# Where z's factors are loaded from, and in what steps z is squared and split, in an FP32 encoder block

## The chip, the core and the metric

The kernel runs on one core of a Trainium2 chip. The metric is the device time of one execution in microseconds. The kernel before took 1945.86 us, the median of three runs (1943.88 to 1946.81).

## The reference, cut to what matters

One layer of an encoder block on 512 positions of width 2048, all in float32. The change lies in its last part, the MLP with a squared ReLU:

```python
m = rms_norm(h, mlp_pre_gain[l])
z = jnp.square(jax.nn.relu(jnp.einsum("bsd,df->bsf", m, w_up[l])))
z = jnp.einsum("bsf,fd->bsd", z, w_down[l])
h = h + rms_norm(z, mlp_post_gain[l])
```

w_up is 2048 x 8192 and w_down 8192 x 2048. Ahead of it stand a projection w_in, two causal convolutions with gates, a LayerNorm, and a projection w_out with a norm.

## The kernel before

**Float32 by parts.** Each operand is split into a high part (a copy rounded to fp32r, made by ACT, L235 for weights) and a low part (the value less the high part, made by DVE, L239), and a block's product is three matmuls: high by low, low by high, high by high.

**Seven products for eight.** Most of w_out, w_up and w_down is multiplied by a scheme of the Strassen-Winograd kind: for two tiles of a weight and two halves of the positions, seven products of sums take the place of eight ("a seven"). The weight sums are DVE's (L163 for w_up, L195 for w_down). For w_up a product is 24 matmuls 128x256 (L292), and `by_seven` runs them in the order r11, t2, t1, r21, t3, r22, t4. p1 (the product r11) is copied out of its bank by ACT (L341, `tmp<-bank`); DVE forms u = p1 + t2 and v = u + t1 (L333, `tmp<-tmp,bank`); the sum into the upper half of c2 (L333, `slot<-tmp,bank`) reads the bank of t3, the "seventh", onto which t4 is then accumulated, so that t4 cannot begin before that sum is done. w_up's first eight tiles are done plainly ("plain pairs", two tiles each, evacuated by `plain_z`), the other 56 as 28 sevens. For w_down, `wide_seven` runs chunks 1 to 7 with two sevens each, a product of 24 matmuls 128x512 (L928), and chunk 0 plainly at the end.

**Order of the work.** The order is the program's. `product` first takes its weights: `take` prepares those of the next products ahead (weight sums, L235, L239). Then `run_pending` issues what has been put in the list `pending`: evacuations of the product before and steps of z. Then come the matmuls. Each engine works through its own instructions in that order.

**z.** The output of a pair of tiles (`zt`, 128x1024) goes to `keep_z`, which puts steps into the list `z_jobs`: Relu, Square and the high part in one step on ACT (L783, L784, L789), then the store of the high part (a DMA on ACT's queue, L804) with the low part (DVE, L333 `slot<-slot,slot`), then the store of the low part with z's own sums (three DVE instructions, not for the first chunk), and the same split and stores for those sums. `up_product` takes one step a product, two when more than six wait. In the first seven of w_up each product also takes two of the eight "late sums": splits by ACT and DVE of 128x256 (L94, L95) which t4's right side needs.

**Factors.** A chunk of z (4 pairs of tiles) is read back from DRAM as factors, t1, t2, r11, t3, r22, t4, r21 in the order of use, each in a high and a low tile of 512 KB (`load_factor`, L893: 14 loads for each of chunks 1 to 7 and 8 for chunk 0). They are issued by SP, on whose queue stand also all loads of raw weights (L122) and of w_down's last blocks of a seven (L207). A tile's place comes from a pool of 43 slots that weights, factors and z share; a load waits for its place. The first chunk's factors are issued at two points of the last `by_seven` and after it; each later chunk's in the second seven of the chunk before, `after` a product.

The profile's names are those of the pools: `raw` a raw weight, `slot` a 4 KB place, `tmp` a scratch tile, `bank` a PSUM bank.

Of the kernel before, what the change touches and what calls it, by code (L numbers as in the profile page):

```python
# [10 lines left out]
AF = mybir.ActivationFunctionType  # L11
# [16 lines left out]
N_UP = FF // P  # L28
# [30 lines left out]
def encoder_block(  # L59
    ctx: ExitStack, tc: tile.TileContext, x, par, gain, w_in, w_out, w_up, w_down, out  # L60
):
    nc = tc.nc
# [239 lines left out]
    def full_tile(parts, moving):  # L302
        ps = bank()
        products(ps, [(block(parts[k // HALF], k % HALF), both(moving[k])) for k in range(KT)])
        return ps
# [30 lines left out]
    def run_pending():  # L336
        while pending:
            pending.popleft()()

    def evacuate(f, *args):  # L340
        pending.append(lambda: f(*args))  # L341
# [11 lines left out]
    def product(right, blocks, onto=None):  # L353
        (part,) = W.take(1, 3)
        run_pending()
        ps = bank(TOK) if onto is None else onto
        products(ps, [(block(part, i), right(i)) for i in range(blocks)], onto=onto is not None)
        return ps

    def by_seven(product, c1, c2, done1, done2, step=lambda n: None):  # L360


        p1, u, v = scratch(TOK), scratch(TOK), scratch(TOK)
        first = product("r11")
        evacuate(nc.scalar.activation, p1, first, AF.Copy)
        evacuate(add, u, p1, product("t2"))
        evacuate(add, v, u, product("t1"))
        product("r21", first)
        evacuate(nc.scalar.activation, c1[:, lower], first, AF.Copy)
        seventh = product("t3")  # L370
        evacuate(add, c2[:, upper], v, seventh)
        evacuate(step, 1)
        evacuate(add, c1[:, upper], v, product("r22"))
        evacuate(done1, c1)
        evacuate(step, 3)
        product("t4", seventh)
        evacuate(add, c2[:, lower], u, seventh)
        evacuate(done2, c2)
# [22 lines left out]
    class Sum:  # L401
# [3 lines left out]
        def add(self, t):  # L405
            if self.total is None:
                self.total = new(stats, [P, self.cols], F32, "sum")
                nc.gpsimd.tensor_copy(self.total, t)
            else:
                nc.gpsimd.tensor_tensor(self.total, self.total, t, op=ALU.add)  # L410
# [182 lines left out]
    for kind, j, m in in_plan[START:]:  # L593
# [3 lines left out]
        ps = full_tile(parts, u)  # L597
# [48 lines left out]
    for m in range(START, OUT_SEVEN[0]):  # L646
        parts = W.take(2, 2)
        run_pending()
        ps = full_tile(parts, mixed)
        evacuate(keep_output, m, ps, scratch())  # L650
    for m in OUT_SEVEN:
        by_seven(
            lambda name, onto=None: product(mixed_factor[name], HALF, onto),
            *(scratch() for _ in range(2)),
            *((lambda c, m=n: keep_output(m, c, c)) for n in (m, m + 1)),
        )
# [111 lines left out]
    WIDE_ORDER = ("t1", "t2", "r11", "t3", "r22", "t4", "r21")  # L768
# [4 lines left out]
    )  # L773
    z_jobs = deque()

    def keep_z(n, zt):


        c, i = divmod(n, PAIRS)
        made = {}  # L780

        def squared():
            nc.scalar.activation(zt, zt, AF.Relu)  # L783
            nc.scalar.activation(zt, zt, AF.Square)  # L784
            high(zt, 0)

        def high(value, g):
            made["hi", g] = slot([P, 4, TOK], F32R)
            nc.scalar.activation(  # L789
                made["hi", g].rearrange("p f w -> p (f w)"),  # L790
                value.rearrange("p a b -> p (a b)"), AF.Copy,
            )

        def rest(value, g):
            made["lo", g] = slot([P, 4, TOK], F32R)
            add(
                made["lo", g].rearrange("p f w -> p (f w)"),
                value.rearrange("p a b -> p (a b)"),
                made["hi", g].rearrange("p f w -> p (f w)").bitcast(F32), ALU.subtract,
            )  # L800

        def store(g, h):
            part = made["lo" if h else "hi", g]
            nc.scalar.dma_start(z_parts[c, g, h, i], part.bitcast(F32))  # L804

        def sums():
            t = made["t"] = slot([P, 4, TOK])
            q = zt.rearrange("p a (b w) -> p (a b) w", b=2)
            add(t[:, :2, :], q[:, 1::2, :], q[:, :2, :], ALU.subtract)
            add(t[:, 2, :], q[:, 3, :], t[:, 0, :], ALU.subtract)  # L810
            add(t[:, 3, :], q[:, 2, :], t[:, 2, :], ALU.subtract)

        z_jobs.append([squared])
        z_jobs.append([lambda: store(0, 0), lambda: rest(zt, 0)])
        if c == 0:
            z_jobs.append([lambda: store(0, 1)])
            return
        z_jobs.append([lambda: store(0, 1), sums])
        z_jobs.append([lambda: high(made["t"], 1)])
        z_jobs.append([lambda: store(1, 0), lambda: rest(made["t"], 1)])  # L820
        z_jobs.append([lambda: store(1, 1)])

    def z_job(n):
        for _ in range(min(n, len(z_jobs))):
            pending.extend(z_jobs.popleft())

    t12, t3, t4 = [], [], []
# [17 lines left out]
    def last_right_sum(i):  # L845
        split(t4[i // 4][:, i % 4, :], *both(mlp_in[2 * i], upper))
# [11 lines left out]
    def plain_z(n, pss, zt):  # L858

        for i, ps in enumerate(pss):  # L860
            nc.scalar.activation(zt[:, i, :], ps, AF.Copy)
        keep_z(n, zt)

    for n in range(START // 2):
        evacuate(lambda n=n: plain_z(n, pss[2 * n : 2 * n + 2], slot([P, 2, S])))
    n = HALF // (UP_PLAIN - START)
    for m in range(START, UP_PLAIN):
        parts = W.take(2, 2)
        run_pending()
        ps = full_tile(parts, mlp_in)  # L870
# [7 lines left out]
    late_sums = deque(range(HALF))  # L878

    def up_product(name, onto=None):  # L880
        for _ in range(2):
            if late_sums:
                pending.append(lambda i=late_sums.popleft(): last_right_sum(i))
        z_job(2 if len(z_jobs) > 6 else 1)
        return product(right_factor[name], HALF, onto)

    factors = {}
# [1 line left out]
    def load_factor(c, name):  # L889
        f = FACTORS.index(name)  # L890
        for h in range(2):
            t = factors[c, name, h] = slot([P, PAIRS, TOK], F32R)
            nc.sync.dma_start(  # L893
                t.rearrange("p i w -> p (i w)").bitcast(F32),
                z_dram.rearrange("p (n w) -> n p w", w=PAIRS * TOK)[((c * 2 + f // 4) * 4 + f % 4) * 2 + h],
            )

    def load_first(n):
        for name in WIDE_ORDER[3 * (n == 3) : 3 + (n == 3)]:
            load_factor(1, name)  # L900

    for m in range(UP_PLAIN, N_UP, 2):
        zt = slot([P, 2, S])
        by_seven(
            up_product,
            zt[:, 0, :],
            zt[:, 1, :],
            lambda c: None,
            lambda c, m=m, zt=zt: keep_z(m // 2, zt),
            load_first if m == N_UP - 2 else lambda n: None,  # L910
        )


# [21 lines left out]
    def right_blocks(c, name, i):  # L935
        return [factors[c, name, h][:, i, :] for h in range(2)]

    def wide_seven(c, t, after):


# [16 lines left out]
        for q, (name, group, to, first) in enumerate((  # L957
            ("t1", "p5", "c2 upper", True),
            ("t2", "p6", "c1 upper", True),
            ("r11", "p1", "all but c1 lower", True),  # L960
            ("t3", "p6", "c2 upper", False),
            ("r22", "p5", "c1 upper", False),
            ("t4", "p6", "c2 lower", True),
            ("r21", "p1", "c1 lower", True),
        )):
            z_job(1)
            parts = W.take(2, 4)
            run_pending()
            if group not in banks:
                banks[group], onto = [bank() for _ in range(2)], False  # L970
            else:
                onto = True
            for j, ps in enumerate(banks[group]):
                for i in range(PAIRS):
                    wide(
                        ps, right_blocks(c, name, i), j, parts[i // 2], i % 2,
                        i == 0 and not onto, i == PAIRS - 1, True,
                    )
                evacuate(accumulate, c == 1 and first, sums[to][j], ps)
            after(q)  # L980

    run_pending()
    for name in WIDE_ORDER[4:]:
        load_factor(1, name)
    for c in range(1, N_CHUNK):
        following = WIDE_ORDER if c + 1 < N_CHUNK else FACTORS[:4]
        c_next = (c + 1) % N_CHUNK

        def after(q):
            if q > 0 and q - 1 < len(following):  # L990
                load_factor(c_next, following[q - 1])

        for t in range(0, N_WIDE, 2):
            wide_seven(c, t, after if t == 2 else lambda q: None)
        if c_next:
            load_factor(c_next, following[-1])

    def wide_tile(t, c, blocks, step):

# [140 lines left out]
    for b in range(TB):  # L1140
        gained = {}
        for t in range(N_WIDE):
            run_pending()
            ps = bank()
# [90 lines left out]
```

## Time and profile before

| | us |
|---|---|
| median of three runs | 1945.86 |
| the profiled execution | 1949.1 |
| its span in the trace | 1947.4 |
| mean granted clock of TensorE in it | 0.993 |

In the trace the stage of w_up's sevens lies from 715.8 us to 1295.1 us, and w_down's from 1294.9 us on. A row of a timeline gives the start from the span's start, the duration, the engine, the line, what is written and read, and in brackets the idle time ahead of it and what ended it. SPq and ACTq are the engines' DMA issues.

### The profile page before, as it was taken

The numbers are of one execution on the slowest core, as the hardware profiler recorded it, in microseconds if no ns is written. First come the engines' busy times: TensorE is split into PE (matmuls) and PEld (weight loads), VectorE is DVE, ScalarE is ACT, GpSimd is POOL, SyncE is SP. The second block draws the span as 40 slices with busy tenths as digits, with TensorE's granted clock in tenths as the row PEclk, the third lists the DMA queues.
The fourth block names the chain that finished last, engine by engine and source line by source line (L and its number), as shares of the span: only waits on it lengthen the run. The fifth ranks groups of instructions, "written<-read, shape, count | busy, mean of one in ns | idle before, by whom it ended". The sixth has DMA issues, their size and how long they took to land.

```text
span 1947.4 us, 27944 instructions
## 1 busy us (share of the span) xinstructions
PE 1908.7 (98%) x11050; PEld 1690.3 (87%) x11050; DVE 1623.2 (83%) x1988; ACT 851.8 (44%) x1058; POOL 81.0 (4%) x70
## 2 busy tenths in 40 slices
PE   8999999999999998999999999989999999999998
PEld 6888888888899788999999999987887888888876
DVE  8799989677785858989989899878789889898748
ACT  6212112252443646555555555546334333343342
POOL 5000010300120000000000000000000000000000
PEclk9999999999999999999999999999999999999999
DMA  7233323222347627666676666787564764755722
GB/s 252 78 112 103 103 93 100 96 89 94 110 142 248 220 81 220 201 208 206 206 218 202 208 206 206 218 290 259 195 238 142 238 225 149 263 186 182 281 87 87
DMA packets 146291, 342.79 MB, mean 176 GB/s; under 512 B 11248, under 2 KB 74864, under 8 KB 146160
## 3 DMA queue, kind: packets, MB, share of 16 engines
q1 hardware_dynamic: 78192, 270.04, 42.8%
q10 hardware_dynamic: 67968, 70.96, 10.8%
q8 instruction: 87, 1.43, 0.3%
q14 instruction: 44, 0.36, 0.0%
HBM read 265.99 MB, written 74.97 MB: 175 GB/s over the span
## 4 chain that ended last, share of the span: by engine, by line
PE 90%; DVE 5%; ACT 2%; DMA 2%; issue 1%; SPq 0%; ACTq 0%; DVEq 0%
PE bank L292 56%; PE bank L928 28%; PE bank L314 2%; PE bank L313 2%; DVE slot L239 2%; PE bank L312 2%; DVE slot L333 1%; DMA raw<-w_down_in 1%; DVE slot L195 1%; ACT slot L235 1%; DMA tmp<-x_in 0%; DMA slot<-z_dram 0%; ACT slot L94 0%; PE bank L1053 0%; DVE slot L98 0%
## 5 line engine op out<-in xcount | busy, mean ns | idle before, releaser
L292 PE MATMUL bank<-slot,slot 128*128 128x256 f32 (+1 forms) x7584 | 1134.5, 312 | 8.4 <-ACT slot L235 5.5
L292 PEld LDWEIGHTS bank<-slot,slot 128*128 128x128 f32 x7584 | 1051.7, 191 | 90.7 <-ACT slot L235 6.7
L928 PE MATMUL bank<-slot,slot 128*128 128x512 f32 x2736 | 628.1, 391 | 10.5 <-DMA slot<-z_dram 4.7
L928 PEld LDWEIGHTS bank<-slot,slot 128*128 128x128 f32 x2736 | 513.4, 188 | 121.7 <-DVE slot L239 5.1
L239 DVE TENSOR_TENSOR slot<-raw,slot 128x1024 fp32r<-128x1024 f32 x336 | 417.4, 1257 | 49.5 <-ACT slot L235 40.3
L235 ACT ACTIVATE slot<-raw 128x1024 fp32r<-128x1024 f32 x336 | 342.4, 1050 | 194.9 <-DVE raw L163 66.7
L235 ACT ACTIVATE slot<-slot 128x1024 fp32r<-128x1024 f32 x208 | 219.4, 1058 | 450.8 <-DVE slot L195 199.1
L239 DVE TENSOR_TENSOR slot<-slot,slot 128x1024 fp32r<-128x1024 f32 x208 | 254.1, 1222 | 29.1 <-PE bank L292 19.2
L503 DVE SCALAR_TENSOR_TENSOR slot<-slot,par_sb,slot 128x512 f32<-128x512 f32 x240 | 163.0, 746 | 0.0
L333 DVE TENSOR_TENSOR slot<-slot,bank 128x512 f32<-128x512 f32 x208 | 134.3, 681 | 14.1 <-PE bank L928 14.1
L333 DVE TENSOR_TENSOR slot<-slot,slot 128x1024 fp32r<-128x1024 f32 (+2 forms) x128 | 104.6, 823 | 41.3 <-ACT slot L789 39.4
L94 ACT ACTIVATE slot<-tmp 128x512 fp32r<-128x512 f32 (+1 forms) x40 | 21.9, 583 | 155.5 <-DVE tmp L536 117.6
L312 PE MATMUL bank<-slot,slot 128*128 128x512 f32 (+1 forms) x216 | 81.1, 376 | 6.2 <-ACT slot L94 6.2
L314 PE MATMUL bank<-slot,slot 128*128 128x512 f32 (+1 forms) x216 | 81.2, 376 | 2.9 <-DVE slot L98 2.9
L313 PE MATMUL bank<-slot,slot 128*128 128x512 f32 (+1 forms) x216 | 81.0, 375 | 1.9 <-DVE slot L239 1.9
L195 DVE TENSOR_TENSOR slot<-slot,raw 128x1024 f32<-128x1024 f32 x28 | 34.3, 1225 | 57.2 <-DMA raw<-w_down_in 56.6
L789 ACT ACTIVATE slot<-slot 128x1024 fp32r<-128x1024 f32 x60 | 63.4, 1056 | 1.0
L410 POOL TENSOR_TENSOR sum<-sum,tmp 128x512 f32<-128x512 f32 x35 | 59.6, 1704 | 94.6 <-ACT tmp L414 93.4
L312 PEld LDWEIGHTS bank<-slot,slot 128*128 128x128 f32 x216 | 41.8, 194 | 13.2 <-ACT slot L94 6.2
L314 PEld LDWEIGHTS bank<-slot,slot 128*128 128x128 f32 x216 | 41.8, 193 | 10.9 <-DVE slot L98 4.1
L313 PEld LDWEIGHTS bank<-slot,slot 128*128 128x128 f32 x216 | 41.7, 193 | 9.8 <-DVE slot L239 2.3
L333 DVE TENSOR_TENSOR tmp<-tmp,bank 128x256 f32<-128x256 f32 x76 | 31.7, 417 | 17.9 <-PE bank L292 17.9
(98 smaller groups left out, 868.1 us busy)
## 6 DMA issues: line engine op xcount, KB each, us to landing
raw<-w_up_in SPq DMA_DIRECT2D x128, 512.0 KB, 4.5
z_dram<-slot ACTq DMA_DIRECT2D x120, 512.0 KB, 3.4
slot<-z_dram SPq DMA_DIRECT2D x106, 512.0 KB, 6.5
raw<-w_down_in SPq DMA_DIRECT2D x100, 512.0 KB, 4.5
raw<-w_in_in SPq DMA_DIRECT2D x76, 512.0 KB, 4.3
raw<-w_out_in SPq DMA_DIRECT2D x32, 512.0 KB, 4.1
slot<-w_down_in SPq DMA_DIRECT2D x28, 512.0 KB, 4.8
tmp<-x_in SPq DMA_DIRECT2D x16, 256.0 KB, 5.0
```

The lines of the kernel that those rows point to most:

```text
L195: nc.vector.tensor_tensor(out, a, b, op=op)
L235: nc.scalar.activation(hi, value, AF.Copy)
L239: nc.vector.tensor_tensor(lo, value, hi.bitcast(F32), op=ALU.subtract)
L292: nc.tensor.matmul(ps, s, m, start=n == 0 and not onto, stop=n == len(todo) - 1, skip_group_check=onto)
L312: nc.tensor.matmul(ps[:, cols], hi, mhi, start=first, stop=False)
L313: nc.tensor.matmul(ps[:, cols], lo, mhi, start=False, stop=False)
L314: nc.tensor.matmul(ps[:, cols], hi, mlo, start=False, stop=last)
L333: add = lambda out, a, b, op=ALU.add: nc.vector.tensor_tensor(out, a, b, op=op)
L410: nc.gpsimd.tensor_tensor(self.total, self.total, t, op=ALU.add)
L503: nc.vector.scalar_tensor_tensor(out=acc, in0=g[:, k : k + S], scalar=w, in1=acc, op0=ALU.mult, op1=ALU.add)
L789: nc.scalar.activation(made["hi", g].rearrange("p f w -> p (f w)"), value.rearrange("p a b -> p (a b)"), AF.Copy,)
L928: matmul = lambda a, b, first=False, last=False: nc.tensor.matmul(ps, a, b, start=first, stop=last, skip_group_check=onto)
```

## The change

Three things change.

First, `load_factor` issues on the GpSimd (POOL) queue, no longer on SP, and earlier: t1 and t2 ahead of product r21 of the last seven of w_up, r11 ahead of t3, t3 ahead of r22, r22 ahead of t4, and t4 and r21 behind it; each later chunk's factors one product earlier than before.

Second, Relu, Square and the high part of z are each a step of their own, so there are eight steps in place of six; of the first eight tiles the Relu is done when they are evacuated (`plain_z`, AF.Relu in place of AF.Copy).

Third, `up_product` takes no step of z as long as late sums are left, which is through the first four products of the first seven, and after that two steps when more than four wait.

```diff
+    first_factors = {"r21": ("t1", "t2"), "t3": ("r11",), "r22": ("t3",), "t4": ("r22",)}
+    def last_product(name, onto=None):
+        for f in first_factors.get(name, ()):
+            load_factor(1, f)
+        return up_product(name, onto)
...
-            nc.sync.dma_start(
+            nc.gpsimd.dma_start(
...
-        def squared():
-            nc.scalar.activation(zt, zt, AF.Relu)
-            nc.scalar.activation(zt, zt, AF.Square)
-            high(zt, 0)
...
-        z_jobs.append([squared])
+        if not positive:
+            z_jobs.append([lambda: nc.scalar.activation(zt, zt, AF.Relu)])
+        z_jobs.append([lambda: nc.scalar.activation(zt, zt, AF.Square)])
+        z_jobs.append([lambda: high(zt, 0)])
         z_jobs.append([lambda: store(0, 0), lambda: rest(zt, 0)])
...
-            nc.scalar.activation(zt[:, i, :], ps, AF.Copy)
-        keep_z(n, zt)
+            nc.scalar.activation(zt[:, i, :], ps, AF.Relu)
+        keep_z(n, zt, True)
...
     def up_product(name, onto=None):
-        for _ in range(2):
-            if late_sums:
+        if late_sums:
+            for _ in range(2):
                 pending.append(lambda i=late_sums.popleft(): last_right_sum(i))
-        z_job(2 if len(z_jobs) > 6 else 1)
+        else:
+            z_job(2 if len(z_jobs) > 4 else 1)
         return product(right_factor[name], HALF, onto)
...
-            if q > 0 and q - 1 < len(following):
-                load_factor(c_next, following[q - 1])
+            if q < len(following):
+                load_factor(c_next, following[q])
...
-        if c_next:
-            load_factor(c_next, following[-1])
```

From line 360 on, the lines of the changed kernel differ: Relu, Square, high part and store of z are L807, L808, L782 and L797, a factor's load is L890, `plain_z` is L857.

How the instructions stand now. On ACT, in one of the steady sevens near the end of w_up, before (L235 a weight's high part, L341 p1's copy, L783 Relu, L784 Square, L789 the high part of z, L804 its stores):

```order
L235 ACTIVATE slot_12279<-slot_12145 128x1024
L341 ACTIVATE tmp_12244<-bank_12253 128x256
L783 ACTIVATE slot_11999<-slot_11999 128x1024
L784 ACTIVATE slot_11999<-slot_11999 128x1024
L789 ACTIVATE slot_12290<-slot_11999 128x1024
L235 ACTIVATE slot_12317<-raw_12041 128x1024
L804 DMA z_dram<-slot_12290 128x4x256
L235 ACTIVATE slot_12350<-raw_12112 128x1024
```

and the same place now:

```order
L235 ACTIVATE slot_12275<-slot_12141 128x1024
L341 ACTIVATE tmp_12240<-bank_12249 128x256
L807 ACTIVATE slot_11995<-slot_11995 128x1024
L808 ACTIVATE slot_11995<-slot_11995 128x1024
L235 ACTIVATE slot_12311<-raw_12037 128x1024
L782 ACTIVATE slot_12316<-slot_11995 128x1024
L797 DMA z_dram<-slot_12316 128x4x256
L235 ACTIVATE slot_12346<-raw_12108 128x1024
```

The next weight's high part has moved from behind z's high part to between it and Square. In the first seven, on ACT, before (L94 the late sums):

```order
L94 ACTIVATE slot_5081<-slot_5584 128x256
L783 ACTIVATE slot_5528<-slot_5528 128x1024
L784 ACTIVATE slot_5528<-slot_5528 128x1024
L789 ACTIVATE slot_5885<-slot_5528 128x1024
L804 DMA z_dram<-slot_5885 128x4x256
L235 ACTIVATE slot_5916<-slot_5780 128x1024
L341 ACTIVATE tmp_5864<-bank_5890 128x256
L94 ACTIVATE slot_5127<-slot_5584 128x256
L94 ACTIVATE slot_5302<-slot_5584 128x256
```

and now:

```order
L94 ACTIVATE slot_5081<-slot_5584 128x256
L235 ACTIVATE slot_5909<-slot_5780 128x1024
L341 ACTIVATE tmp_5864<-bank_5883 128x256
L94 ACTIVATE slot_5127<-slot_5584 128x256
L94 ACTIVATE slot_5302<-slot_5584 128x256
L235 ACTIVATE slot_5947<-raw_5617 128x1024
```

The three instructions of z and its store are gone from ahead of the weight's high part and p1's copy; they come after the second copy (L341) of this seven. On SP's queue, at the start of w_down, before (L893 factors, L207 and L122 weights):

```order
L207 DMA slot_12668<-w_down_in 128x1024
L893 DMA slot_12676<-z_dram 128x1024
L893 DMA slot_12678<-z_dram 128x1024
L893 DMA slot_12680<-z_dram 128x1024
L893 DMA slot_12682<-z_dram 128x1024
L893 DMA slot_12684<-z_dram 128x1024
L893 DMA slot_12686<-z_dram 128x1024
L207 DMA slot_12716<-w_down_in 128x1024
L122 DMA raw_12718<-w_down_in 128x1024
L893 DMA slot_12726<-z_dram 128x1024
```

and now:

```order
L207 DMA slot_12680<-w_down_in 128x1024
L207 DMA slot_12720<-w_down_in 128x1024
L122 DMA raw_12722<-w_down_in 128x1024
L122 DMA raw_12814<-w_down_in 128x1024
L122 DMA raw_12821<-w_down_in 128x1024
```

The factors no longer stand between the weights; all 106 are on POOL's queue, behind its sums for the norms and ahead of the two instructions that build an identity for the tail.

More of the change, by code (lines that the diff above doesn't have):

```diff
@@ L358, in product, with by_seven @@
         return ps
-    def by_seven(product, c1, c2, done1, done2, step=lambda n: None):
+    def by_seven(product, c1, c2, done1, done2):
         p1, u, v = scratch(TOK), scratch(TOK), scratch(TOK)
@@ L371, in by_seven @@
         evacuate(add, c2[:, upper], v, seventh)
-        evacuate(step, 1)
         evacuate(add, c1[:, upper], v, product("r22"))
         evacuate(done1, c1)
-        evacuate(step, 3)
         product("t4", seventh)
@@ L774, in encoder_block, with keep_z @@
     z_jobs = deque()
-    def keep_z(n, zt):
+    def keep_z(n, zt, positive=False):
         c, i = divmod(n, PAIRS)
         made = {}
-        def squared():
-            nc.scalar.activation(zt, zt, AF.Relu)
-            nc.scalar.activation(zt, zt, AF.Square)
-            high(zt, 0)
         def high(value, g):
@@ L896, in load_factor @@
             )
-    def load_first(n):
-        for name in WIDE_ORDER[3 * (n == 3) : 3 + (n == 3)]:
-            load_factor(1, name)
+    first_factors = {"r21": ("t1", "t2"), "t3": ("r11",), "r22": ("t3",), "t4": ("r22",)}
[3 more added lines that the diff above has]
+        return up_product(name, onto)
     for m in range(UP_PLAIN, N_UP, 2):
@@ L904, in encoder_block @@
         by_seven(
-            up_product,
+            last_product if m == N_UP - 2 else up_product,
             zt[:, 0, :],
@@ L909, in encoder_block @@
             lambda c, m=m, zt=zt: keep_z(m // 2, zt),
-            load_first if m == N_UP - 2 else lambda n: None,
         )
@@ L982, in encoder_block @@
     run_pending()
-    for name in WIDE_ORDER[4:]:
+    for name in WIDE_ORDER[5:]:
         load_factor(1, name)
```

## The prediction

> **What bounds the kernel now.** I read the engine table first, then the list of what TensorE waits for, then two tables of stretches, and last the engines' timelines around the three places that these name.
>
> ```profile
> PE 1908.7 (98%) x11050; PEld 1690.3 (87%) x11050; DVE 1623.2 (83%) x1988; ACT 851.8 (44%) x1058; POOL 81.0 (4%) x70
> ```
> ```profile
> PE bank L292 <- ACT slot L235: 5.5, 1, 5.5
> PE bank L928 <- DMA slot<-z_dram: 4.7, 1, 4.7
> PE bank L928 <- DVE slot L333: 2.8, 3, 1.2
> PE bank L928 <- ACT slot L918: 2.3, 1, 2.3
> PE bank L292 <- ACT tmp L341: 2.0, 1, 2.0
> PE bank L292 <- DVE slot L333: 0.9, 1, 0.9
> ```
> ```profile
> 720.00:760.00 40.00, 32.51 (x241) 32.14 (x240) 30.76 (x38) 26.91 (x33) 0.00 (x0) 0.87 0.72 218
> 760.00:800.00 40.00, 40.00 (x335) 40.00 (x335) 36.23 (x42) 23.06 (x26) 0.00 (x0) 1.00 0.66 207
> 1280.00:1320.00 40.00, 32.86 (x189) 28.64 (x187) 27.96 (x30) 18.51 (x21) 0.00 (x0) 0.91 0.91 325
> 1320.75:1395.80 75.05, 75.05 (x331) 62.16 (x332) 62.08 (x61) 39.18 (x48) 0.00 (x0) 1.00 0.72 243
> ```
> TensorE is busy 98%, so the change can only touch the waits (total, times, longest) and what its granted clock loses behind them. In the tables of stretches the columns are time, then PE, weight load, DVE, ACT and POOL busy with counts, then clock, DMA share and GB/s. **First seven of w_up, about 724 to 742**: 241 matmuls where the next 40 us hold 335; 241 take 28.8 us at that rate, so 11.2 are lost, 7.5 in the two waits (2.0 and 5.5) and 3.7 in a clock of 0.87. **Start of w_down, about 1291 to 1320**: 0.9, 4.7 and 2.3 us of waits, and more lost clock. Whatever else the change does, these are about 21 us, 1.1% of the run.
>
> The steady sevens of w_up (742 to 1291) show no wait, but that is not the whole story:
> ```profile
> 783.38 0.41 DVE L333 TENSOR_TENSOR slot<-tmp,bank 128x256 f32<-128x256 f32 x1
> 1255.41 1.21 DVE L163 TENSOR_TENSOR slot<-raw,slot 128x1024 f32<-128x1024 f32 x1
> 1261.21 1.23 DVE L333 TENSOR_TENSOR slot<-slot,slot 128x1024 fp32r<-128x1024 f32 x1 [1.48 <-ACT slot L789]
> 1270.14 0.41 DVE L333 TENSOR_TENSOR slot<-tmp,bank 128x256 f32<-128x256 f32 x1
> ```
> ```profile
> 1256.72 1.06 ACT L235 ACTIVATE slot<-slot 128x1024 fp32r<-128x1024 f32 x1 [1.69 <-DVE slot L163]
> 1257.68 0.36 ACT L341 ACTIVATE tmp<-bank 128x256 f32<-128x256 f32 x1
> 1257.95 1.05 ACT L783 ACTIVATE slot<-slot 128x1024 f32<-128x1024 f32 x1
> 1259.03 1.06 ACT L784 ACTIVATE slot<-slot 128x1024 f32<-128x1024 f32 x1
> 1260.12 1.06 ACT L789 ACTIVATE slot<-slot 128x1024 fp32r<-128x1024 f32 x1
> 1261.08 1.04 ACT L235 ACTIVATE slot<-raw 128x1024 fp32r<-128x1024 f32 x1
> ```
> ```profile
> 750.00:820.00 70.00, 70.00 (x586) 70.00 (x585) 1.00 0.71 219
> 1200.00:1270.00 70.00, 70.00 (x583) 69.80 (x582) 1.00 0.66 204
> ```
> The rows at 783.38 and 1270.14 are the same instruction, 24 sevens apart: the sum into c2's upper half, which has to be read out of its bank before product t4 may write there. 486.76 / 24 = 20.28 us a seven. A seven has 168 matmuls; at 335 in 40 us they take 20.06, and late in the stage the same 70 us hold 3 fewer than early. So TensorE is already held, by some 0.1 us a seven, to a **loop of DVE and ACT**: weight sum (L163, DVE), its high part (L235), p1's copy (L341), Relu, Square, high part of z (L783, L784, L789, all ACT), then z's low part on DVE at 1261.21, which waited 1.48 us for that high part; from there DVE works without a pause through the sum of 1270.14 to the next L163. Nothing in this loop waits for TensorE.
>
> **The change, part by part.**
>
> *z's steps in the first seven.* While late sums remain, four products long, no z step is issued. By that DVE loses, ahead of its sum into c2 (before, at 741.24), three z splits, and the waits for ACT:
> ```profile
> DVE slot L95 <- ACT slot L94: 3.5, 3, 2.5
> DVE slot L333 <- ACT slot L789: 2.7, 1, 2.7
> 741.24 0.41 DVE L333 TENSOR_TENSOR slot<-tmp,bank 128x256 f32<-128x256 f32 x1
> 725.99 10.33 PE L292 MATMUL bank<-slot,slot 128*128 128x256 f32 x72 [2.01 <-ACT tmp L341]
> 741.80 6.43 PE L292 MATMUL bank<-slot,slot 128*128 128x256 f32 x35 [5.48 <-ACT slot L235]
> ```
> Splits back to back cost 1.14 each (1.23 less the overlap): 3.4. With 6.2 of waits the sum starts near 731.6 and ends at 732.0. TensorE, without its two waits and the half clock behind the first (of the 3.7 us about 1.7), would be at t4 at 741.80 - 5.48 - 2.01 - 1.7 = 732.6. So the sum is just in time: t4 starts 9.2 us earlier, and the half clock behind the second wait goes too.
>
> *The backlog.* The four plain pairs' z, left over, are worked off at two steps a product over the next sevens (their four Relus, 1.06 each, are now done by the evacuation). Seven two: 15 long DVE instructions at 1.14 to 1.26 and 5 short ones at 0.34 are about 19, with 1 to 1.5 of waits for ACT 20.3, as TensorE's 20.1. Seven three has two z of its own kind: 14 long (16.2), two groups of sums at 1.6, 5 short (1.7), about 21, and two waits for the high parts of some 2 and 1.2: 24.3 us. Its sum into c2 then ends near 732.0 + 20.3 + 24.3 = 776.6, started at 776.2, 7.2 us before the 783.38 of before.
>
> *z's steps in the steady sevens.* Relu and Square now stand in one product and the high part in the next, and the next weights' L235 (the row at 1261.08) gets between Square and the high part. In the loop this is one ACT instruction more: the high part starts not 1.09 after Square (1259.03 to 1260.12) but two of ACT's steps after it, 2 x 0.95 (0.96 from 1260.12 to 1261.08). That is **0.82 us a seven**, and since DVE has no pause behind it and its order is unchanged, the sum into c2 and t4 come 0.82 later every seven: period 21.1. From seven three to the last there are 25: 20.5. The stage then ends 20.5 - 7.2 = **13.3 us later** than before. ACT is at 23.06 of 40 us there and DVE at 36.23, so a share of busy time does not show this; only the loop does. Queued behind the high part are z's low part and, on DVE, all of the next seven's weights; its store, on ACT's queue, is 0.82 later too, which nobody waits for, as z is read back chunks later. If t4 had slack it would cost nothing: the first rival.
>
> *The factor loads at the start of w_down.*
> ```profile
> 1276.96 1.43 SPq L122 DMA_DIRECT2D raw<-w_down_in  x2
> 1282.80 12.14 SPq L893 DMA_DIRECT2D slot<-z_dram  x6
> 1295.03 0.39 SPq L207 DMA_DIRECT2D slot<-w_down_in  x1
> 1295.51 0.43 SPq L122 DMA_DIRECT2D raw<-w_down_in  x1
> 1302.85 1.23 DVE L195 TENSOR_TENSOR slot<-slot,raw 128x1024 f32<-128x1024 f32 x1 [9.88 <-DMA raw<-w_down_in]
> 1305.27 13.20 PE L928 MATMUL bank<-slot,slot 128*128 128x512 f32 x48 [4.71 <-DMA slot<-z_dram]
> ```
> SP issues in order: six factor loads take from 1282.80 to 1294.94, since each waits for its place, and only then come two weight loads. The raw weight of 1295.51 lands at 1302.85, where DVE has been idle 9.9 us, and L195, its high part and the second product follow, at 1305.27; the profile names a factor load as the last, but weights and factor arrive together. With the factors on POOL the raw weight is issued when its own place is free, at about 1291 in the time of before: 4.5 us earlier, landing at 1296 to 1299; L195 and L235 take 2.4, so the product could start at 1298 to 1301, and TensorE is ready at 1300.56. Of 4.71 remain 0 to 1. The 48 matmuls behind it took 13.20 where 331 in 75.05 make 10.9: 2.3 of half clock, gone. DVE, earlier by as much, has the bank's evacuation (the 2.3 of L918) ready. Sum 4.7 - 0.5 + 2.3 + 2.3, rounded down for what the last z's single steps may still hold up: **-8.5**, between -9 and 0 (second rival).
>
> *The later chunks.* Loads start one product earlier and off SP's queue; the three waits of together 2.8 are for weights whose places free at the same point as before. I take -0.8, between -2.8 and +2.
>
> *A load issued by POOL.* The trace has none. Nearest rows: SP's issue of a transfer, and POOL's own work.
> ```profile
> slot<-z_dram SPq DMA_DIRECT2D x106, 512.0 KB, 6.5
> L410 POOL TENSOR_TENSOR sum<-sum,tmp 128x512 f32<-128x512 f32 x35 | 59.6, 1704 | 94.6 <-ACT tmp L414 93.4
> ```
> Between 0.39 and 1.70 us each; POOL has nothing else (its busy time is 0.00 in all four stretches above), and one product of w_down, 24 matmuls of 0.227, lasts 5.4 us for two loads. Only beyond 2.7 would it fall behind. I take the row of the same operation, 0.39: off the path, at nothing; at 1.70 the first six end some 10 us after the first, still before 1294.94. Behind the loads, which wait on POOL for their places, stand only the identity's two instructions for the tail. It may cost DVE, though: third rival.
>
> **Sum** against the profiled execution's 1949.1: +13.3 - 8.5 - 0.8 = +4.0, so 1953.1. The runs' median is 1945.86, 0.17% below that execution; on its scale 1949.9, and I say **1949.5**. The start, the stage before w_up and the tail are untouched.
>
> **Rivals.**
> *The loop gives nothing away* (t4 has slack, or ACT's added step is made up): the stage ends as TensorE's 20.1 allows, so the 20.5 are not paid: 1949.5 - 20.5 = 1929. For it: no wait is shown in 742 to 1291. Against: the 3 missing matmuls, and 1.48 us of DVE waiting on that very high part.
>
> *The start of w_down is bound by bandwidth, not by SP's order* (the slower side). In 1280 to 1320 the DMA share is 0.91 at 325 GB/s. If the fourteen early loads share it with the raw weight, that lands as late as before once it is later than about 1300.56 - 2.4 = 1298.2, and the 8.5 us stay lost: 1958. Against: the issue time 4.5 us earlier. The Trainium skill, "DMA: Bandwidth & Descriptors", section "Issuing engines are not separate DMA queues", speaks for this rival: it says that transfers started by several engines run on the same 16 DMA engines and interleave, so that only issue time is saved. By it, only SP's queueing would go; no row here shows a load from POOL, so the trace does not yet decide.
>
> *POOL's work holds DVE up.*
> ```profile
> 579.71 1.89 POOL L410 TENSOR_TENSOR sum<-sum,tmp 128x512 f32<-128x512 f32 x1 [0.36 <-ACT tmp L414]
> 580.36 2.32 DVE L239 TENSOR_TENSOR slot<-raw,slot 128x1024 fp32r<-128x1024 f32 x1
> ...
> L239 DVE TENSOR_TENSOR slot<-slot,slot 128x1024 fp32r<-128x1024 f32 x208 | 254.1, 1222 | 29.1 <-PE bank L292 19.2
> ```
> Beside a POOL operation L239 takes 2.32 instead of 1.22. Were each of 106 loads to cost DVE up to 1.1 us, a chunk of 75 us (14 loads) would lose 15 where DVE has 75.05 - 62.08 = 13.0 idle: 2 to 3 us a chunk over seven chunks, about 20, so 1970. Against: that POOL operation reads and writes SBUF; a load's issue reads none. The Trainium skill, "SBUF — State Buffer", section "Who interferes with whom", limits it so: a DVE instruction with two SBUF inputs contends with a GpSimd instruction that reads SBUF, not with one that only writes it. By that rule this rival's cost would be nothing; the pair of rows agrees with its first half, and no row here bears on the second.
>
> **How the numbers follow.** Forecast 0.62 (its own range 1943 to 1956, from +-1.5 for seven three, +-1.5 for 25 times 0.82, and -2.8 to +2 in the later chunks); loop gives nothing 0.14; bandwidth 0.14; POOL 0.10. A measurement of this kernel tells 0.2%, 3.9 us, from no change. The forecast's share is 0.03 faster, 0.38 same, 0.21 slower; the first rival is faster, the two others slower: 0.17, 0.38, 0.45. The range leaves out the first rival and the upper half of the third: 1936 to 1962.
>
> **What would show it.** The waits 2.0 and 5.5 on L292 near 724 and 736 gone, and the clock there 1.00. A wait of 0.8 to 1.0 us on DVE L333 once a seven, some 24 times, the period 21.1, and L235 between L808 and L782 in ACT's timeline. The second product of w_down with a wait below 1.5 us. DVE's L239 at 1.22 in w_down: if above, the third rival. What would make it wrong most: no such wait in the steady sevens.

## The result, and the profile after

The changed kernel takes 1971.42 us (median of four runs, 1968.76 to 1973.77) against 1946.34 before (median of four, of which three lie within 1943.88 to 1946.81 and one, unexplained, took 6726.01). The ratio, over fast runs alone, is 1.0128, with a 95% interval of 1.0116 to 1.0141. It is 25 us slower. The prediction said 1949.5, within 1936 to 1962, so it missed. The profiled execution's span went from 1947.4 to 1969.7 us, by 22.3.

The page's engine table and groups of the changed kernel (busy time and mean duration, then the idle time ahead and what ended it), and the list of TensorE's waits (total, times, longest):

```profile
PE 1912.3 (97%) x11050; PEld 1690.8 (86%) x11050; DVE 1623.2 (82%) x1988; ACT 848.3 (43%) x1054; POOL 136.3 (7%) x176
L239 DVE TENSOR_TENSOR slot<-slot,slot 128x1024 fp32r<-128x1024 f32 x208 | 254.2, 1222 | 30.7 <-PE bank L292 20.8
L890 POOL DMA_DIRECT2D slot<-z_dram x106 | 56.3, 531 | 1181.5 <-PE bank L292 694.6
slot<-z_dram POOLq DMA_DIRECT2D x106, 512.0 KB, 5.6
```
```profile
PE bank L292 <- DVE slot L333: 23.6, 26, 3.7
PE bank L928 <- DVE slot L333: 7.6, 5, 1.8
...
PE bank L928 <- ACT slot L918: 2.3, 1, 2.3
PE bank L292 <- ACT slot L235: 1.8, 1, 1.8
```

The waits of 4.7 and 2.0 us are gone, as forecast; that of 5.5, ahead of the first seven's t4, was to go too, and 1.8 of it is left. In their place stand 26 waits on L333 in w_up, 23.6 us, and in w_down the waits on L333 grew from 2.8 to 7.6. Here are one seven of the steady part in ACT's and DVE's timelines, and two rows of TensorE's:

```profile
1254.31 1.06 ACT L235 ACTIVATE slot<-slot 128x1024 fp32r<-128x1024 f32 x1 [1.60 <-DVE slot L163]
1255.28 0.37 ACT L341 ACTIVATE tmp<-bank 128x256 f32<-128x256 f32 x1
1255.54 1.05 ACT L807 ACTIVATE slot<-slot 128x1024 f32<-128x1024 f32 x1
1256.62 1.06 ACT L808 ACTIVATE slot<-slot 128x1024 f32<-128x1024 f32 x1
1257.59 1.04 ACT L235 ACTIVATE slot<-raw 128x1024 fp32r<-128x1024 f32 x1
1258.53 1.04 ACT L782 ACTIVATE slot<-slot 128x1024 fp32r<-128x1024 f32 x1
```
```profile
1259.61 1.23 DVE L333 TENSOR_TENSOR slot<-slot,slot 128x1024 fp32r<-128x1024 f32 x1 [2.19 <-ACT slot L782]
1268.55 0.41 DVE L333 TENSOR_TENSOR slot<-tmp,bank 128x256 f32<-128x256 f32 x1
```
```profile
1269.11 20.38 PE L292 MATMUL bank<-slot,slot 128*128 128x256 f32 x168 [0.70 <-DVE slot L333]
1290.19 2.02 PE L292 MATMUL bank<-slot,slot 128*128 128x256 f32 x15 [0.70 <-DVE slot L333]
```

This is the loop of the prediction: the weight's L235 at 1257.59 stands between Square and the high part, z's low part on DVE waits 2.19 us where it waited 1.48, the sum into c2 (1268.55) is later by as much, and TensorE waits 0.70 us for it once a seven (0.8 to 1.0 was forecast). From 1269.11 to 1290.19 are 21.08 us.

To see where the time stands, the trace of each kernel is cut by the starts of matmuls: from the first seven's first matmul to w_down's first, then 100 matmuls of w_down, the next 1900, and the rest to the end of the span.

| us | w_up's sevens | first 100 | next 1900 | rest |
|---|---|---|---|---|
| before | 579.7 | 32.3 | 434.5 | 185.7 |
| changed | 599.8 | 26.8 | 439.7 | 187.9 |
| difference | +20.1 | -5.5 | +5.2 | +2.2 |
| predicted | +13.3 | -8.5 | -0.8 (with the rest) | |

Each row is one execution. The first seven starts between 712.6 and 716.2 us in the 14 traces of this study, so stretches are compared, not whole spans.

### The profile page after: what moved, and what is told of

It reads as the page before. It is cut to its first block, busy times and chain, and to the rows that moved or that the text cites. A ratio compares the mean times of both kernels' runs of the same rounds, so it can differ in the third digit from the quotient of the medians.

```text
span 1969.7 us, 28062 instructions
## 1 busy us (share of the span) xinstructions
PE 1912.3 (97%) x11050; PEld 1690.8 (86%) x11050; DVE 1623.2 (82%) x1988; ACT 848.3 (43%) x1054; POOL 136.3 (7%) x176
## 4 chain that ended last, share of the span: by engine, by line
PE 30%; DVE 16%; ACT 8%; issue 6%; DMA 2%; DVEq 0%; ACTq 0%; SPq 0%
PE bank L928 25%; DVE slot L239 5%; DVE slot L163 5%; PE bank L292 5%; ACT slot L235 4%; DVE slot L333 4%; DMA raw<-w_down_in 2%; ACT slot L782 1%; ACT slot L807 1%; DVE raw L163 1%; DVE slot L195 1%; DVE tmp L333 1%; DMA z_dram<-slot 0%; ACT tmp L341 0%; DMA raw<-w_up_in 0%
## 5 line engine op out<-in xcount | busy, mean ns | idle before, releaser
L292 PE MATMUL bank<-slot,slot 128*128 128x256 f32 (+1 forms) x7584 | 1137.5, 312 | 25.4 <-DVE slot L333 23.6
L292 PEld LDWEIGHTS bank<-slot,slot 128*128 128x128 f32 x7584 | 1052.3, 192 | 110.1 <-ACT slot L782 24.3
L239 DVE TENSOR_TENSOR slot<-raw,slot 128x1024 fp32r<-128x1024 f32 x336 | 416.3, 1253 | 59.0 <-ACT slot L235 40.5
L235 ACT ACTIVATE slot<-raw 128x1024 fp32r<-128x1024 f32 x336 | 344.8, 1051 | 211.7 <-DVE raw L163 67.8
L235 ACT ACTIVATE slot<-slot 128x1024 fp32r<-128x1024 f32 x208 | 219.6, 1059 | 459.3 <-DVE slot L163 185.7
L239 DVE TENSOR_TENSOR slot<-slot,slot 128x1024 fp32r<-128x1024 f32 x208 | 254.2, 1222 | 30.7 <-PE bank L292 20.8
L333 DVE TENSOR_TENSOR slot<-slot,slot 128x1024 fp32r<-128x1024 f32 (+2 forms) x128 | 104.6, 823 | 61.8 <-ACT slot L782 57.5
L333 DVE TENSOR_TENSOR slot<-slot,bank 128x512 f32<-128x512 f32 x208 | 133.6, 681 | 7.2 <-PE bank L928 7.2
L890 POOL DMA_DIRECT2D slot<-z_dram x106 | 56.3, 531 | 1181.5 <-PE bank L292 694.6
L94 ACT ACTIVATE slot<-tmp 128x512 fp32r<-128x512 f32 (+1 forms) x40 | 21.9, 583 | 155.3 <-DVE tmp L534 117.3
L195 DVE TENSOR_TENSOR slot<-slot,raw 128x1024 f32<-128x1024 f32 x28 | 34.3, 1225 | 54.0 <-DMA raw<-w_down_in 53.6
L782 ACT ACTIVATE slot<-slot 128x1024 fp32r<-128x1024 f32 x60 | 62.9, 1048 | 0.3
```

The costliest lines, as they stand in the source:

```text
L235: nc.scalar.activation(hi, value, AF.Copy)
L239: nc.vector.tensor_tensor(lo, value, hi.bitcast(F32), op=ALU.subtract)
L292: nc.tensor.matmul(ps, s, m, start=n == 0 and not onto, stop=n == len(todo) - 1, skip_group_check=onto)
L333: add = lambda out, a, b, op=ALU.add: nc.vector.tensor_tensor(out, a, b, op=op)
L782: nc.scalar.activation(made["hi", g].rearrange("p f w -> p (f w)"), value.rearrange("p a b -> p (a b)"), AF.Copy,)
```

## The experiments

Three theories run through the expectations. A: the loop of DVE and ACT costs some 20 us in w_up, and the loads cost the rest in w_down. B: in w_down's later chunks it is the point of the program at which a pair of factors is loaded that makes the raw weight late. C: the pool of 43 places is the bound where work has been put off or moved forward.

**z's steps alone, and the loads alone.** The first kernel is the one before with the z part of the diff and nothing of `load_factor`; the second is the changed kernel with the z part taken back.

> Only the z part of the change: single steps, no z step while late sums are left, the factor loads on SP as before. Theory A (the loop of DVE and ACT in w_up costs 20 us, the loads cost the rest): t4 of the last seven starts near 1312 as in the changed kernel, a wait of 0.70 once a seven; the stage of w_down as in the kernel before, with its 4.7 us wait: 1966 us. Rival (the loads, or their places, cause the steady waits): the waits of 0.70 are gone and the time is 1940 to 1946.

> Only the loads part: factors on POOL and earlier, z's steps as before. Theory A: w_up as before, period 20.28; the 4.7 us wait at the start of w_down gone (5 to 7 us gained), and given back in the later chunks by five waits of 1.4 to 1.8 on L333 (7 us): 1945 to 1950. Rival (the later chunks' waits come from z's late steps): those waits as before, together about 2.8, so 1938 to 1941.

Measured: z's steps alone 1966.77 us (ratio 1.0095, 1.0078 to 1.0112), the loads alone 1954.61 (1.0032, 1.0023 to 1.0042); the kernel before, run beside them, took 1947.35. TensorE's waits with z's steps alone, then with the loads alone:

```profile
PE bank L292 <- DVE slot L333: 24.6, 27, 3.9
...
PE bank L927 <- DMA slot<-z_dram: 5.2, 1, 5.2
PE bank L927 <- DVE slot L333: 3.0, 4, 1.1
```
```profile
PE bank L929 <- DVE slot L333: 7.1, 5, 1.8
...
PE bank L929 <- DVE slot L239: 3.4, 1, 3.4
```

So the two parts stand apart. z's steps make w_up 599.9 us and leave w_down as it was (31.6, 434.9, 185.8). The loads leave w_up as it was (580.0) and make the five waits in w_down's later chunks (438.2 in the third column). Theory A holds as to where each part acts. The loads alone came out some 5 us above the upper end of what was expected, since at the normal pace of the sevens the start of w_down gains only 1.3 us (31.0 in the second column), not 5.

**The order on ACT.** In the changed kernel, the high part goes into Square's step and an empty step follows, so that nothing else moves. In the traces DVE's 1988 instructions stand in the same order, and on ACT only high parts of z (L782) have moved, in the steady sevens by one place.

```diff
-        z_jobs.append([lambda: nc.scalar.activation(zt, zt, AF.Square)])
-        z_jobs.append([lambda: high(zt, 0)])
+        z_jobs.append([lambda: nc.scalar.activation(zt, zt, AF.Square), lambda: high(zt, 0)])
+        z_jobs.append([])
```

> The changed kernel with the high part of z in the step of Square and an empty step behind it, so that the next weight's L235 stands behind the high part again and DVE's order is unchanged. Theory A: the steady waits of 0.70 vanish, period 20.28, the time falls by 0.80 for each of 24 to 25 sevens, 19 to 20 us, to 1951 to 1952. Rival (places, or POOL, hold the sevens up): period stays 21.08 and the time 1971.

Measured: 1952.40 us, 19.0 less than the changed kernel. TensorE's waits in w_up, and its timeline in the steady part:

```profile
PE bank L292 <- DVE slot L333: 6.6, 3, 4.9
```
```profile
1239.72 45.53 PE L292 MATMUL bank<-slot,slot 128*128 128x256 f32 x376
```

Of 26 waits 3 remain, and 376 matmuls, more than two sevens, run without one; the period is 20.28. In the traces w_up's sevens take 578.6 us, 21.2 less than in the changed kernel, and the start of w_down gives 4.3 of it back (31.1 in place of 26.8). The place of one ACT instruction was worth 19 us of 1971.

**The queue, and the product.** Four kernels have z's steps as before and differ only in where the factors are loaded. The one before with POOL's queue alone, at the old points:

```diff
-            nc.sync.dma_start(
+            nc.gpsimd.dma_start(
```

> The kernel before with the factor loads on POOL and nothing else, so at the same points of the program. Theory A (two queues in parallel slow the raw weight that DVE waits for): the start of w_down gains about 5, the later chunks lose: its raw weight takes 8.5 us to land instead of 7.5 and waits of 1.4 to 1.8 on L333 stand in four or five chunks: 1945 to 1950. Rival (it is the earlier product that costs): the later chunks wait as before, 2.8 together, and the time is 1939 to 1942.

Then the loads part with the later chunks' loads put back by one product:

```diff
-            if q < len(following):
-                load_factor(c_next, following[q])
+            if q > 0 and q - 1 < len(following):
+                load_factor(c_next, following[q - 1])
...
+        if c_next:
+            load_factor(c_next, following[-1])
```

> z's steps as before; all factors on POOL, the first chunk's early as in the change, the later chunks' after the products of before. Theory B (a later chunk's pair of loads one product earlier coincides with the raw weight that DVE waits for, and that alone costs the 4 us): matmuls 100 to 2000 of w_down take 434.5 to 435 us as before, not 438 to 440; the first 100 take 31 as with the whole loads part; 1945 to 1949. Rival (it is the first chunk's early loads that carry on into the later chunks): 438 and more.

And the loads part, early as in the change, on SP's queue:

```diff
-            nc.gpsimd.dma_start(
+            nc.sync.dma_start(
```

> z's steps as before; factors as early as in the change, but on SP's queue. Theory B (the point of the program, not the queue): matmuls 100 to 2000 take 438 or more, as on POOL; the first 100 more than 32, since the early loads wait on SP ahead of weights: 1950 to 1958. Rival (POOL's queue beside SP's is what costs): 434 to 435 in the middle.

| | time (ratio, interval) | first 100 | next 1900 | rest | raw weight lands after, mean |
|---|---|---|---|---|---|
| before (SP, old points) | 1946 to 1948 | 32.3 | 434.5 | 185.7 | 7.80 |
| POOL, old points | 1943.34 (0.9978, 0.9969 to 0.9988) | 28.9 | 434.7 | 185.8 | 7.90 |
| POOL, early | 1954.61 (1.0032) | 31.0 | 438.2 | 187.3 | 8.64 |
| POOL, only the first chunk early | 1945.34 (0.9991, 0.9981 to 1.0001) | 30.8 | 432.6 | 186.0 | 7.42 |
| SP, early | 1959.32 (1.0067, 1.0047 to 1.0086) | 33.6 | 434.9 | 188.4 | 7.26 |

The last column is the time from the issue of the raw weight to the start of L195 on DVE, which waits for it, over five later chunks. This time decides over TensorE's wait: of the 25 chunks of the five kernels, none whose weight landed within 7.3 us has one, and each whose weight took 7.8 or more has one, of 0.5 to 1.8. In every one of these, TensorE starts again 19.5 to 19.6 us after L195, with DVE's work between, at whose end TensorE wants a bank.

The queue alone makes the kernel faster, by 0.2%: with no factors ahead of the weights on SP the start of w_down gains 3.4 us. The later chunks' waits stay as they were (3.1 us in three), as the rival expected; the time is 1.3 above the rival's range. The early points take the gain back and more, and putting only the later chunks' loads back by one product brings 9.3 us (1954.61 to 1945.34), so on POOL's queue theory B holds.

On SP's queue the early point costs as well, though the column of the next 1900 matmuls (434.9) does not show it: three of the five later chunks wait for 1.74, 1.34 and 1.59 us, and the last of these stands behind matmul 2000, in the rest (188.4 against 185.7). With the rest, the later chunks lose 3.1 us on SP and 5.3 on POOL. On SP more is lost ahead of w_down and in its first matmuls, since weights stand behind loads that wait for places (w_up's sevens take 585.0). The changed kernel's queues around one raw weight, POOL's, SP's and DVE's, and its stretches:

```profile
1697.03 1.15 POOL L890 DMA_DIRECT2D slot<-z_dram  x2 [4.54 <-PE bank L928]
1702.70 1.06 POOL L890 DMA_DIRECT2D slot<-z_dram  x2 [4.52 <-PE bank L928]
```
```profile
1695.07 2.14 SPq L207 DMA_DIRECT2D slot<-w_down_in  x2
1697.64 0.33 SPq L122 DMA_DIRECT2D raw<-w_down_in  x1
```
```profile
1705.93 1.23 DVE L195 TENSOR_TENSOR slot<-slot,raw 128x1024 f32<-128x1024 f32 x1 [6.88 <-DMA raw<-w_down_in]
```
```profile
1697.64:1700.00 2.36, 2.36 (x12) 1.97 (x11) 1.41 (x3) 0.24 (x1) 0.53 (x1) 1.00 0.73 215
1700.00:1702.50 2.50, 2.50 (x13) 2.07 (x12) 0.00 (x0) 0.00 (x0) 0.00 (x0) 1.00 1.03 387
1702.50:1705.90 3.40, 3.40 (x17) 2.81 (x16) 0.00 (x0) 0.00 (x0) 1.05 (x2) 1.00 0.91 349
```

The pair of factor loads and the raw weight start within 0.6 us, and while the weight is under way the DMA engines are nearly full (the share, last but one, is 1.03 and 0.91) and DVE does nothing. In this chunk the weight takes 8.29 us, about as before (8.34); the mean is longer by the other four chunks.

The two L207 rows show what else has moved: the first of these loads had waited 9.1 us for a place. It is issued 2.2 to 2.6 us ahead of the raw weight in all five chunks, where the kernel before issued it 5.3 to 5.8 us ahead:

```profile
1671.68 0.33 SPq L207 DMA_DIRECT2D slot<-w_down_in  x1
1677.08 0.38 SPq L207 DMA_DIRECT2D slot<-w_down_in  x1
1677.51 0.42 SPq L122 DMA_DIRECT2D raw<-w_down_in  x1
```

So the early factors take places, and the weight's block that lacks one is loaded beside the raw weight. Early on SP both cases occur in one kernel: with that load 2.9 us ahead (three chunks) the raw weight takes 7.9 to 8.3 us and TensorE waits, with it 5.7 and 6.8 ahead (two chunks) it takes 6.3 and 5.6 and TensorE does not. It is not the only cause: in the kernel before, the raw weight takes from 7.0 to 8.5 us with that load 5.3 to 5.8 ahead.

**Places.** The changed kernel with one more place, paid for with scratch tiles:

```diff
-    tmp = pool("tmp", 8)
+    tmp = pool("tmp", 6)
...
-    slots = pool("slots", 43)
+    slots = pool("slots", 44)
```

> The changed kernel with 44 places for slots in place of 43, paid for with 6 scratch tiles in place of 8. Theory C (in the second seven of w_up DVE waits 2.4 us for a place that t4 frees and 1.5 for one that a store of z frees, which the prediction left out): one more place takes part of these waits away, and t4 of seven two starts 1 to 2.5 us earlier after t4 of seven one than the 24.1 us of the changed kernel; the steady period stays 21.08. Rival (DVE has too much to do there): 24.1 as before.

Measured in a single run: 1954.87 us, 16.5 less than the changed kernel. From t4 of the first seven to t4 of the second are 21.2 us in place of 24.1 (2.8 less, a little over what was expected). The waits of DVE in the changed kernel between 728 and 763 us, then with the one place more:

```profile
732.94 1.23 DVE L239 TENSOR_TENSOR slot<-slot,slot 128x1024 fp32r<-128x1024 f32 x1 [1.60 <-PE bank L292]
736.89 1.23 DVE L333 TENSOR_TENSOR slot<-slot,slot 128x1024 fp32r<-128x1024 f32 x1 [2.40 <-PE bank L292]
748.07 1.23 DVE L333 TENSOR_TENSOR slot<-slot,slot 128x1024 fp32r<-128x1024 f32 x1 [0.75 <-ACT slot L782]
750.82 1.23 DVE L239 TENSOR_TENSOR slot<-raw,slot 128x1024 fp32r<-128x1024 f32 x1 [1.52 <-DMA z_dram<-slot]
762.50 1.23 DVE L333 TENSOR_TENSOR slot<-slot,slot 128x1024 fp32r<-128x1024 f32 x1 [2.37 <-ACT slot L782]
```
```profile
731.45 1.23 DVE L239 TENSOR_TENSOR slot<-slot,slot 128x1024 fp32r<-128x1024 f32 x1 [2.62 <-PE bank L292]
735.41 1.23 DVE L239 TENSOR_TENSOR slot<-slot,slot 128x1024 fp32r<-128x1024 f32 x1 [1.27 <-PE bank L292]
745.34 1.23 DVE L333 TENSOR_TENSOR slot<-slot,slot 128x1024 fp32r<-128x1024 f32 x1 [0.76 <-ACT slot L782]
758.23 1.23 DVE L333 TENSOR_TENSOR slot<-slot,slot 128x1024 fp32r<-128x1024 f32 x1 [2.38 <-ACT slot L782]
```

These instructions read nothing that TensorE or a store writes, so their waits at 732.94, 736.89 and 750.82 were for places: what DVE writes may go into a tile only once TensorE has read its old content, or a store has taken it away. With 44 places DVE comes to the first of them some 2.5 us sooner and waits longer (2.62), but of the two later ones, 3.9 us, only 1.27 remains. t4 of the second seven starts 4.3 us earlier. The steady period stays 21.09. What was not expected: the five waits of w_down's later chunks are gone as well (431.5 us for the 1900 matmuls, the raw weight lands after 7.10), though the pair of loads still starts within 0.5 us of the raw weight. So the coincidence of the factors with it is not enough to make the weight late; it took the lack of a place too. With 44 places the first L207 is issued 5.9 us ahead of the raw weight again, as in the kernel before. No run moved that load alone.

**Versions that might beat both.** The first takes the kernel before with POOL's queue, no z step while late sums are left, Relu, Square and high part in one step, and the plain pairs' Relu in their evacuation as in the change (the diff shows the second point):

```diff
...
-        for _ in range(2):
-            if late_sums:
+        if late_sums:
+            for _ in range(2):
                 pending.append(lambda i=late_sums.popleft(): last_right_sum(i))
-        z_job(2 if len(z_jobs) > 6 else 1)
+        else:
+            z_job(2 if len(z_jobs) > 6 else 1)
...
```

> The kernel before with the loads on POOL at their points of before, no z step while late sums are left, Relu, Square and high part in one step, two steps when more than six wait, the plain pairs' Relu in their evacuation. Theory A (the steady order of ACT decides): period 20.28 from seven three on, the first sevens 1 to 4 us better than before, w_down as with the queue alone: 1939 to 1943. Rival (the backlog costs whatever the order): t4 of seven three no earlier than before, 1943 to 1946.

Measured: 1944.22 us (0.9985, 0.9975 to 0.9994), above the first expectation and within the rival's range: the period is 20.28 as it should be, but t4 of the third seven starts 68.5 us after the first seven, where it was 69.0, and the rival said no earlier. Holding the steps back gains 5.3 us at the first t4 (21.3 in place of 26.6) and loses them again by the third: the backlog costs what the delay gave.

Then four with 44 places and 6 scratch tiles: the kernel before, the loads part alone, the kernel with the high part in Square's step, and the one just named.

> The kernel before with 44 places for slots and 6 scratch tiles in place of 43 and 8. Theory C (places set when weights and factors can be made and loaded): t4 of the first sevens earlier, waits in w_down's later chunks gone; 1940 to 1944, the steady period 20.28 unchanged. Rival (the place helped the changed kernel only, with its early loads): 1945 to 1948.

> Only the loads part of the change, with 44 places and 6 scratch tiles. Theory C: the later chunks' five waits, 7 us with 43 places, are mostly gone (matmuls 100 to 2000 take 431 to 433 us, as in the changed kernel with 44 places): 1940 to 1946. Rival (the early loads themselves collide with the raw weight): 437 to 439 as with 43 places, 1950 to 1955.

> The changed kernel with the high part in the step of Square (and the empty step), and with 44 places and 6 scratch tiles. Theories A and C together: the steady period 20.28 and t4 of seven three some 4 us earlier than in the changed kernel, w_down as with 44 places: 1955 less 20, 1933 to 1937, faster than the kernel before. Rival (the two do not add up, since DVE is the next bound in the first sevens): 1938 to 1944.

> Loads on POOL at their points of before, no z step while late sums are left, Relu, Square and high part in one step, 44 places and 6 scratch tiles. Theories A and C: 1934 to 1940. Rival (without the early loads the start of w_down stays late): 1940 to 1944.

| 44 places | time (ratio, interval) | w_up's sevens | first 100 | next 1900 |
|---|---|---|---|---|
| before | 1943.26 (0.9984, 0.9974 to 0.9993) | 576.6 | 34.2 | 431.3 |
| loads part | 1942.34 (0.9975, 0.9966 to 0.9985) | 576.6 | 30.6 | 433.7 |
| changed, high part in Square's step | 1938.63 (0.9959, 0.9944 to 0.9974) | 573.2 | 30.6 | 431.8 |
| POOL's queue, steps held back | 1939.78 (0.9963, 0.9950 to 0.9976) | 574.5 | 30.0 | 432.7 |

All four are faster than the kernel before, by 0.2 to 0.4%; the first, second and fourth lie in the ranges expected. The early loads, which cost 7 us with 43 places, cost nothing with 44, and this, over ten runs, repeats what the single run showed. In the loads part's trace one later chunk still has a wait, of 1.95 us: its raw weight took 9.2 us to land, with the first L207 5.9 us ahead, and why is not known. The third has the lowest time of the study, 32.8 us below the changed kernel with two small edits (the fourth is not clear of it: their intervals overlap), and its waits of TensorE are few:

```profile
PE bank L292 <- DVE slot L333: 6.1, 4, 3.5
...
PE bank L928 <- ACT slot L918: 3.7, 1, 3.7
...
PE bank L928 <- DVE slot L333: 0.6, 1, 0.6
```

The two gains, 19 and 16.5, come to nearly their sum: 1935.9 if they added, 1938.6 measured, a little above the range of 1933 to 1937 that was expected, and inside its rival's.

## Why the prediction was wrong

**The loop in the steady sevens: right.** Predicted 0.82 us a seven; the period went from 20.28 to 21.08, with a wait of 0.70, and taking the instruction out of the loop gave 19.0 us back (21.2 in w_up's sevens, where 20.5 was put down). The prediction's first rival, that the loop gives nothing away, is out, and the view that showed it was not a wait of TensorE (before there was none) but the constant distance of one instruction of DVE from itself.

**The first seven and the backlog: a gain of 7.2 us was put down, 0.8 was there.** The sum into c2 was to end at 732.0; it started at 734.08, after 1.60 us in which L239 waited for a place. Seven two was to take 20.3 us of DVE, with 1 to 1.5 of waits for ACT; its waits were 4.8, of which 3.9 for places and 0.75 for ACT, and it took 24.1. Seven three took 24.9, close to the 24.3 put down. t4 of the third seven thus starts 68.2 us after the first seven's start, not some 62, where it was 69.0 before. The step that failed is "with 1 to 1.5 of waits for ACT": it counted DVE's work and its inputs, but not where its outputs go. With 44 places t4 of the third seven starts after 64.2 us, so the one place is worth 4.0 of the 6.4 us that were missing; the rest was not tested.

**The start of w_down: the wait of 4.7 went, the gain was 5.5, not 8.5.** The 2.3 us behind L918 stayed. And even the 5.5 belong to the slow sevens: at the normal pace the same loads gain 1.3 (1.2 in the kernel with the high part in Square's step). With the loads alone the raw weight is issued when it was forecast, at 1291.27, but takes 10.9 us to land, at 1302.16, where 5 to 8 was put down. Here the rows are the queue and DVE of that kernel:

```profile
1291.27 0.39 SPq L122 DMA_DIRECT2D raw<-w_down_in  x1
```
```profile
1302.16 1.23 DVE L195 TENSOR_TENSOR slot<-slot,raw 128x1024 f32<-128x1024 f32 x1 [8.62 <-DMA raw<-w_down_in]
```

The second rival, bandwidth, was therefore much of the truth: a weight that is issued 4.2 us earlier among fourteen loads lands only 0.7 earlier. From 1291 to 1302 us the DMA share was 1.04 in that kernel and 0.97 before. The Trainium skill, "DMA: Bandwidth & Descriptors", section "Issuing engines are not separate DMA queues", says that transfers started by different engines run on the same 16 DMA engines and interleave, so that only the time to start them is saved. The runs agree only in part: with the queue alone, and the loads later, 3.4 us were gained. In that kernel SP's two L207 loads ahead of the raw weight began at 1280.67, not 1288.09, so that it was issued at 1286.73 and had landed by 1296.16. Here too the early loads held a weight's load back.

**The later chunks: -0.8 was put down, +7.4 was there.** This is the largest miss. The step that failed reads "the three waits of together 2.8 are for weights whose places free at the same point as before". For the raw weight that was so: it is issued 0.6 to 0.7 us into the same product, in one chunk 1.0. It was not so for the L207 load ahead of it, which now waited for its place. And the raw weight landed 0.9 us later (8.71 in place of 7.80), so that the three waits grew and in two chunks that had been just in time a wait of 1.4 appeared: 7.6 us in place of 2.8, and some 1.6 more for matmuls at half pace behind the longest. Of the range given, -2.8 was the sum of the old waits going; for the other end, +2, no row was given.

**POOL's work holding DVE up: out.** L239 takes 1222 ns as before and DVE's busy time is 1623.2 us in both kernels. The Trainium skill, "SBUF — State Buffer", section "Who interferes with whom", has a VectorE instruction with two SBUF inputs contend with a GpSimd instruction that reads SBUF and not with one that only writes it; this agrees, as far as DVE's durations go.

The profiled span grew by 22.3 us where the sum said 4.0. Of the 18.3 between, some 6.4 lie in the backlog, 0.4 in the steady sevens, 3.0 at the start of w_down and 8.2 behind it; 0.2 are ahead of w_up's sevens. So the loop was rightly foreseen and rightly priced, and the gains that were to pay for most of it were not there.

## What to carry to other kernels

A loop between two engines that runs at the pace of the third shows no wait at all; look for an instruction of such a loop at a constant distance from itself, and count an instruction put into it at nearly its whole step (here 0.80 us for a step of 0.95), however idle its engine is. When work is put off, ask where its outputs will go: in a pool without a free tile the backlog waits for readers, not for its own engine. And a load that is started earlier takes a place earlier: ask which other load then lacks one, and measure when the load that is waited for lands.

## What the runs showed of the hardware

A load issued by POOL took 0.53 us of POOL and landed after 5.6 us in the median in the changed kernel. SP's landed after 6.5 in the kernel before and after 5.5 at the early points, so the difference is not shown to be the issuing engine's. Waits of TensorE of 0.7 us, once a seven, left its granted clock at 1.00 (1200 to 1270 us); behind the waits of 3.69, 2.27, 2.11 and 1.84 us of the changed kernel the matmuls ran at half pace for 3 to 6 us (in w_down 0.43 us each in place of 0.23), behind those of 1.81 and 1.70 not. The length of the wait alone does not decide it: behind one of 1.81 with z's steps alone the matmuls ran at half pace, behind one of 2.50 with 44 places they did not. No run was made to find what does.
